# Attention maxima paced two groups ahead with the mask added on VectorE, and retention's dependent steps one projection part later

## The chip, the cores and the metric

The kernel runs on one core of a Trainium2 chip. The metric is device time in microseconds (us) of one launch, the median of three runs; one further run was profiled, and every row below is from it. The engines are named as the profile names them: PE (TensorE matmul; PEld is its weight load), DVE (VectorE), ACT (ScalarE), POOL (GpSimd) and SP, which issues all DMAs.

## What is computed

One decoder layer on 2048 tokens of width 1024, in float32: RMSNorm and one input projection; 8 heads of chunkwise retention beside 8 heads of causal softmax attention with low-rank q and k/v; one output projection with residual; RMSNorm, up-projection, causal depthwise convolution, SiLU gate, down-projection with residual; a last RMSNorm. The two parts that the change touches are, cut short:

```python
# retention, per head and chunk
scores = einsum('bnihd,bnjhd->bnhij', q, k) * decay_mask
o = einsum('bnhij,bnjhe->bnihe', scores, v) + einsum('bnihd,bnhde,hi->bnihe', q, r_prev, xi)
# then group norm over each head and the gate silu(g) * o

# attention, per block of queries
s = (q_nope . k_nope + q_pe . k_pe) * scale
s = where(key_pos <= q_pos, s, finfo(float32).min)
p = softmax(s)                       # needs the maximum of every row of s
o = einsum('bhqk,bkhd->bqhd', p, v)
```

## The kernel before, in words

Every float32 operand is split into a rounded high part and a low part, and a product is three matmuls (`mm3`: high by high, high by low, low by high, lines L72 to L74). Splits are made by ACT (high part, L64) and by POOL or DVE (low part, L68).

The program has four stretches. First norm, latents and the q, k, v rows of attention, which go to HBM. Then retention and attention side by side: this is the stretch that the change touches. Then the output projection, and last the convolution MLP. The scheduler of the language reorders the instructions of each engine by readiness and by the order in which the code emits them; the order that it leaves is fixed in the program.

**Retention** (`ret_stream`, `ret_chunk`) works on 4 head pairs times 8 chunks of 256 tokens, two pairs interleaved. A chunk has 8 projection parts of 6 matmuls (L72 to L74, tile `pm`, one PSUM bank), four for each 128 tokens, and after each four parts DVE rotates q and k out of the bank (L597, L598, L600). Then come 8 dependent steps: the split of q and k (tile `S`, ACT and POOL) with 16 half-size transposes on PE (L619, tile `x`); two score steps (L635, L636, mask L637, split `SC`); two output steps (L661, reduced by L662 into `o`); the state (L671 to L678); the statistics of the norm with the gate (L684, L686 `o<-o,sg`, the small operations L104 to L114, L687); and the two transposes of `o` with the store (L691). The dependent steps of a chunk are emitted between the projection parts of the next chunk, one after each part, the first step after the first part.

**Attention** (`att_stream`, `att_max`, `att_group`) has 32 groups: 8 heads times 4 groups g of 512 queries. `att_max` finds the maxima of a group's rows: 4(g+1) units, each a matmul q by k into the single bank `sm` (L727) and a DVE reduction of that bank (L731). Where the unit holds the diagonal, a second matmul of `unit` and a mask adds the mask in PSUM first (L730). Then the maxima are negated (L734), split (L66, L68), transposed into `sm` (L740) and copied by ACT into rows 96 and 97 of the group's `q` tile (L741), so that the score matmul subtracts them. `att_group` then walks over 4g+4 blocks of 128 keys: scores into `s` (two banks, L759 to L764), two exponentials on ACT (L766, L767), the low part on DVE (L768), the running denominator on POOL (`den`, L773, L777), and two value matmuls (L782, L783). At a group's end POOL adds the output halves (L815, tile `ot`) and splits `den`, and two small matmuls sum it (L788, also in `sm`). A chunk of k and v is loaded and split (ACT and POOL, tiles `k`, `v`) when the first maximum unit needs it.

While group n runs, the maxima of group n+1 are emitted between its steps at the rate units/steps:

```python
            steps, units = 4 * g + 5, 4 * groups[n + 1][1] + 6 if n + 1 < len(groups) else 0
            owed, qn = 0.0, None
            for c in self.att_group(h, g, q):
                owed += units / steps
```

that is 2.0 a step in the group g=0, 1.56 in g=1, 1.38 in g=2 and 0.35 in g=3, whose successor is the small first group of the next head. `side_by_side` interleaves the two streams by their estimated costs; four retention chunks go with one head of attention.

Of the kernel before, what the change touches and what calls it, by code (L numbers as in the profile page):

```python
# [20 lines left out]
P = 128  # L21
D = 1024
# [22 lines left out]


AHEAD = 2
RET_SHARE = .91
ATT_SHARE = .6
LEAD = 9  # L50
# [3 lines left out]
class Block:  # L54
# [387 lines left out]

    def att_pools(self, ctx):
        nc, a, tc = self.nc, self.a, self.tc
        self.kp = ctx.enter_context(tc.tile_pool(name="ak", bufs=5, side="right"))
        self.b1 = b1 = ctx.enter_context(tc.tile_pool(name="a1", bufs=1, side="right"))
        self.b2 = ctx.enter_context(tc.tile_pool(name="a2", bufs=2, side="right"))
        self.b3 = ctx.enter_context(tc.tile_pool(name="a3", bufs=3, side="right"))
        self.pa_m = ctx.enter_context(tc.tile_pool(name="pa_m", bufs=1, space=PSUM, side="right"))
        self.pa_s = ctx.enter_context(tc.tile_pool(name="pa_s", bufs=2, space=PSUM, side="right"))  # L450
        self.pa_o = ctx.enter_context(tc.tile_pool(name="pa_o", bufs=1, space=PSUM, side="right"))
        self.unit = b1.tile([P, P], F32R, name="unit")
        nc.scalar.activation(self.unit, self.ident, AF.Copy)
        m = b1.tile([P, 640], F32R, name="mqk")
        r = self.raw.tile([P, D], F32, name="raw")[:, :640]
        nc.sync.dma_start(r, a["mask_att"])
        nc.scalar.activation(m, r, AF.Copy)
        self.mkq, self.mqk = m[:, 0:384], m[:, 256:640]
        self.ones = b1.tile([P, 2], F32R, name="ones")
        nc.vector.memset(f32(self.ones), 1.0)  # L460

        self.vts = [b1.tile([P, 4, 160], F32R, name=f"v{i}") for i in range(5)]
# [53 lines left out]

    def ret_stream(self):
        nc, a = self.nc, self.a
        hs, pend = {}, None

        def load(ch):
            if ch < 8 and ch not in hs:
                t = hs[ch] = []
                for tt in range(2):
                    h = self.hp.tile([P, 2, KC, P], F32R, name="h")
                    nc.sync.dma_start(f32(h), f32(self.hT_s[2 * ch + tt]))
                    t.append(h)

        for p in (0, 2):
            load(0)  # L530
            for ch in range(8):
                load(ch)
                for j in range(2):
                    if p + j not in self.Wr:
                        for k in range(4):
                            self.ret_weights(p + j, k)
                    it = self.ret_chunk(p + j, ch, self.Wr[p + j], hs[ch])
                    for _ in range(8):
                        yield next(it)
                        if pend is not None:  # L540
                            yield next(pend, 0)
                    if ch == 7:
                        self.next_weights(p + j)
                    if pend is not None:
                        for c in pend:
                            yield c
                    pend = it
                hs.pop(ch)
        for c in pend:
            yield c  # L550

    def att_stream(self):
        groups = [(h, g) for h in range(H) for g in range(4)]
        q = None
        for c, q in self.att_max(*groups[0]):
            yield c
        for n, (h, g) in enumerate(groups):
            nxt = self.att_max(*groups[n + 1]) if n + 1 < len(groups) else iter(())
            steps, units = 4 * g + 5, 4 * groups[n + 1][1] + 6 if n + 1 < len(groups) else 0
            owed, qn = 0.0, None  # L560
            for c in self.att_group(h, g, q):
                owed += units / steps
                while owed >= 1:
                    owed -= 1
                    m = next(nxt, None)
                    if m:
                        c += m[0]
                        qn = m[1]
                yield c
            for m in nxt:  # L570
                qn = m[1]
                yield m[0]
            q = qn
        self.finish()
        yield 450

    def ret_chunk(self, p, ch, W, hs):
        nc, c1, c2, px = self.nc, self.r1, self.r2, self.pr_x
        mm = nc.tensor.matmul
        qk = c2.tile([P, 2, 4, 64], F32, name="qk")  # L580
        vg = c2.tile([P, 2, 256], F32, name="vg")
        V = c2.tile([P, 2, 2, 2, 64], F32R, name="V")
        sg = c2.tile([P, 2, P], F32, name="sg")
        for tt in range(2):
            tok = 2 * ch + tt
            ps = self.pr_m.tile([P, 512], F32, name="pm")
# [18 lines left out]
        th = c1.tile([P, 2, P], F32, name="th")  # L605
# [35 lines left out]
        if ch:  # L641
# [6 lines left out]
        o = c2.tile([P, 4, 64], F32, name="o")  # L648
        for ib in range(2):

            ps = px.tile([P, 512], F32, name="x")
            for x in range(2):
# [12 lines left out]
                axis=AX, op=ALU.add)  # L665
# [12 lines left out]
            nc.vector.tensor_tensor(R, pv[:, :, 64:128], R, op=ALU.add)  # L678
        yield 440

        sq = c1.tile([P, 4, 64], F32, name="gsq")
# [31 lines left out]
    def att_max(self, h, g):  # L713

        nc, b2 = self.nc, self.b2
        q = b2.tile([98, 2, 512], F32R, name="q")
# [3 lines left out]
        mx = b2.tile([P, 4, 4], F32, name="mx")  # L720
# [12 lines left out]
        nm = b2.tile([P, 4], F32, name="nm")  # L733
        nc.vector.tensor_reduce(nm, mx[:, :, :g + 1], axis=AX, op=ALU.max, negate=True)  # L734
# [663 lines left out]
```

## Time and profile before

| | us |
|---|---|
| median of 3 runs | 2969.17 (2965.57 to 2970.82) |
| the profiled run's own time | 2968.21 |
| its span in the trace | 2966.4 |
| PE busy | 2768.4 (93%) |
| DVE busy | 1953.1 (66%) |
| POOL busy | 1957.8 (66%) |
| ACT busy | 1348.3 (45%) |
| PE share of the chain that ended last | 56%, DVE 15%, ACT 7%, POOL 6% |

The span begins with the first instruction and ends with the last; the run's own time has 1.8 us around it. A matmul is pipelined, so its duration is longer than the distance to the next one, and the distance is what it costs. "PEclk" is the share of the full TensorE clock of 2.4 GHz that was granted in a stretch; the lower level is 1.2 GHz.

### The profile page before, as it was taken

What the parts mean: (1) busy time and instruction counts of PE and PEld (TensorE: products, weight loads), DVE (VectorE), ACT (ScalarE), POOL (GpSimd) and SP (SyncE); (2) the same over time, 40 slices, a digit from 0 to 9 for tenths busy, and PEclk for the clock granted to TensorE, in tenths of its full rate; (3) what the DMA queues carried; (4) which work ended last, traced back from release to release, by engine and by line L of the source; (5) the groups of instructions that cost most, each with busy time, mean ns of one, the idle gap of its engine ahead of it and who ended that gap; (6) DMA issues with size and microseconds to landing.
All of it is one profiled execution on the core that took longest, in us unless ns stands there. A gap on an engine that the chain in (4) does not pass through costs nothing.

```text
span 2966.4 us, 37611 instructions
## 1 busy us (share of the span) xinstructions
PE 2768.4 (93%) x12800; PEld 2237.1 (75%) x12800; DVE 1953.1 (66%) x3265; ACT 1348.3 (45%) x2544; POOL 1957.8 (66%) x1478
## 2 busy tenths in 40 slices
PE   7998999988999999989899999989995999999998
PEld 6976777777777777767787777778874888887887
DVE  8765676667666666754458888844266888887243
ACT  5435656555655555551333333333334433333343
POOL 2035656566655556663599999765558999995564
PEclk9999999999999999999899999989997999999999
DMA  7663112223211121326622222264552222224453
GB/s 259 219 209 95 53 55 65 59 70 97 63 54 55 54 65 45 97 88 196 241 94 77 73 85 81 79 228 153 187 192 96 71 79 86 79 74 163 149 193 109
DMA packets 153360, 332.91 MB, mean 112 GB/s; under 512 B 35016, under 2 KB 68296, under 8 KB 147024
## 3 DMA queue, kind: packets, MB, share of 16 engines
q1 hardware_dynamic: 153168, 330.51, 34.1%
q8 instruction: 101, 1.65, 0.2%
q14 instruction: 91, 0.75, 0.1%
HBM read 237.71 MB, written 92.75 MB: 111 GB/s over the span
## 4 chain that ended last, share of the span: by engine, by line
PE 56%; DVE 15%; ACT 7%; issue 6%; POOL 6%; DMA 3%; SPq 0%; POOLq 0%; ACTq 0%; DVEq 0%
PE b L74 10%; PE b L73 10%; PE b L72 10%; PE pm L74 3%; PE pm L72 3%; PE pm L73 3%; DVE w L1137 2%; DVE u L1131 2%; DVE w L1138 2%; PE sm L727 2%; ACT w L1136 2%; PE s L759 2%; PE x L661 2%; DVE w L1163 2%; PE s L764 1%
## 5 line engine op out<-in xcount | busy, mean ns | idle before, releaser
L68 POOL TENSOR_TENSOR w<-raw,w 128x512 fp32r<-128x512 f32 (+2 forms) x315 | 523.2, 1676 | 256.2 <-ACT w L64 243.8
L74 PE MATMUL b<-F,w 128*128 128x512 f32 x1232 | 492.5, 400 | 0.0
L72 PE MATMUL b<-F,w 128*128 128x512 f32 x1232 | 487.7, 396 | 3.8 <-DVE u L1131 3.8
L73 PE MATMUL b<-F,w 128*128 128x512 f32 x1232 | 487.5, 396 | 3.1 <-POOL F L68 3.1
L777 POOL TENSOR_TENSOR den<-den,pc 128x512 f32<-128x512 f32 (+2 forms) x256 | 294.1, 1149 | 207.8 <-ACT pc L766 189.8
L64 ACT ACTIVATE w<-raw 128x512 fp32r<-128x512 f32 (+2 forms) x328 | 214.4, 658 | 348.1 <-PE b L74 179.0
L72 PE MATMUL b<-w 128*128 128x512 f32 x832 | 330.2, 397 | 21.0 <-DVE u L1131 13.0
L74 PE MATMUL b<-w 128*128 128x512 f32 x832 | 328.1, 394 | 1.6 <-POOL w L68 1.5
L73 PE MATMUL b<-w 128*128 128x512 f32 x832 | 328.0, 394 | 0.0
L731 DVE TENSOR_REDUCE mx<-sm 128x1 f32<-128x512 f32 (+2 forms) x320 | 194.1, 607 | 173.8 <-PE sm L727 126.9
L68 DVE TENSOR_TENSOR w<-xr,w 128x512 fp32r<-128x512 f32 x88 | 110.4, 1255 | 284.9 <-ACT w L64 284.9
L72 PEld LDWEIGHTS b<-F,w 128*128 128x128 f32 x1232 | 232.6, 189 | 65.7 <-DVE u L1131 11.0
L73 PEld LDWEIGHTS b<-F,w 128*128 128x128 f32 x1232 | 232.5, 189 | 62.4 <-POOL F L68 3.5
L74 PEld LDWEIGHTS b<-F,w 128*128 128x128 f32 x1232 | 232.4, 189 | 54.5
L768 DVE TENSOR_TENSOR pc<-s,pc 128x512 fp32r<-128x512 f32 (+1 forms) x320 | 197.6, 619 | 99.6 <-ACT s L767 74.6
L1136 ACT ACTIVATE w<-u,cw 128x1024 f32<-128x1024 f32 x88 | 109.5, 1244 | 333.1 <-DVE u L1131 198.5
L1137 DVE SCALAR_TENSOR_TENSOR w<-u,cw,w 128x1024 f32<-128x1024 f32 x88 | 165.7, 1883 | 128.7 <-ACT w L1136 128.7
L766 ACT ACTIVATE pc<-s 128x512 fp32r<-128x512 f32 (+1 forms) x320 | 172.6, 539 | 148.5 <-PE s L764 142.1
L72 PE MATMUL pm<-w,h 128*128 128x512 f32 x512 | 211.1, 412 | 6.3 <-DVE t L598 4.8
L68 POOL TENSOR_TENSOR w<-xr,w 128x512 fp32r<-128x512 f32 x110 | 204.6, 1872 | 9.4 <-ACT w L64 9.4
L74 PE MATMUL pm<-w,h 128*128 128x512 f32 x512 | 206.5, 403 | 0.0
L73 PE MATMUL pm<-w,h 128*128 128x512 f32 x512 | 205.7, 402 | 0.0
(263 smaller groups left out, 6618.6 us busy)
## 6 DMA issues: line engine op xcount, KB each, us to landing
raw<-in_w_down SPq DMA_DIRECT2D x88, 512.0 KB
h<-hT_s SPq DMA_DIRECT2D x32, 1024.0 KB
xr<-in_w_up SPq DMA_DIRECT2D x44, 512.0 KB
raw<-in_w_up SPq DMA_DIRECT2D x44, 512.0 KB
g_s<-w SPq DMA_DIRECT2D x44, 512.0 KB
xr<-g_s SPq DMA_DIRECT2D x88, 256.0 KB
hT_s<-hT SPq DMA_DIRECT2D x16, 1024.0 KB
raw<-in_w_ret SPq DMA_DIRECT2D x16, 512.0 KB
```

Of the source, the lines that this page charges most:

```text
L64: nc.scalar.activation(hi, src, AF.Copy)
L68: eng.tensor_tensor(lo, src, f32(hi), op=ALU.subtract)
L72: mm(out, lhsT=lh, rhs=rh, start=start, stop=False)
L73: mm(out, lhsT=lh, rhs=rl, start=False, stop=False)
L74: mm(out, lhsT=ll, rhs=rh, start=False, stop=stop)
L661: mm(ps[:, x * P:x * P + 256], lhsT=l, rhs=r, start=n == 0, stop=n == len(ops) - 1)
L731: nc.vector.tensor_reduce(mx[:, i, c:c + 1], ps[:, :w], axis=AX, op=ALU.max)
L766: nc.scalar.activation(pc[:, 0, r0:], ps[:, r0:], AF.Exp, scale=ATT_SCALE)
L768: nc.vector.tensor_tensor(pc[:, 1, r0:], ps[:, r0:], f32(pc[:, 0, r0:]), op=ALU.subtract)
L777: nc.gpsimd.tensor_tensor(den[:, r0:], den[:, r0:], hi[:, r0:], op=ALU.add)
L1136: nc.scalar.activation(acc, x[:, 2:1026], AF.Identity, scale=w2, bias=b)
L1137: nc.vector.scalar_tensor_tensor(acc, x[:, 1:1025], w1, acc, op0=ALU.mult, op1=ALU.add)
```

## The change

Four edits. (1) `att_max`: the mask matmul goes; on diagonal units DVE adds the mask and takes the maximum in one `tensor_tensor_reduce`, which writes the sum back to the bank. The mask for it is a float32 tile, filled by a POOL memset and a DMA. (2) `att_stream`: the maxima become one stream over all groups, taken at 1.1 units a step, up to two groups ahead; what a group still lacks at its start is emitted there. `q` and `mx` get three buffers, `k` and `v` six. (3) `ret_stream`: nothing of the chunk before is emitted after the first part, its steps follow after parts 2 to 8, and its last step after part 3 of the chunk after. (4) `ret_chunk`: `qk`, `vg`, `V`, `sg` and `o` go from two buffers to one, and the squares share a tile with `th`.

```diff
+MAX_PACE = 1.1
...
-        self.kp = ctx.enter_context(tc.tile_pool(name="ak", bufs=5, side="right"))
+        self.kp = ctx.enter_context(tc.tile_pool(name="ak", bufs=6, side="right"))
...
+        self.mqk = b1.tile([P, 512], F32, name="mqk")
+        nc.gpsimd.memset(self.mqk, 0.0)
+        nc.sync.dma_start(self.mqk[:, 384:512], a["mask_att"][:, 384:512])
...
-                    for _ in range(8):
+                    for n in range(8):
                         yield next(it)
-                        if pend is not None:
+                        if n and pend is not None:
                             yield next(pend, 0)
+                        if n == 2 and old is not None:
+                            yield next(old, 0)
                     if ch == 7:
                         self.next_weights(p + j)
-                    if pend is not None:
-                        for c in pend:
-                            yield c
-                    pend = it
+                    old, pend = pend, it
...
     def att_stream(self):
         groups = [(h, g) for h in range(H) for g in range(4)]
-        q = None
-        for c, q in self.att_max(*groups[0]):
-            yield c
+        qs, done = {}, set()
+        def maxima():
+            for n, hg in enumerate(groups):
+                while n > self.at + 2:
+                    yield 0
+                for c, qs[n] in self.att_max(*hg):
+                    yield c
+                done.add(n)
+        self.at, mx, owed = 0, maxima(), 0.0
         for n, (h, g) in enumerate(groups):
-            nxt = self.att_max(*groups[n + 1]) if n + 1 < len(groups) else iter(())
-            steps, units = 4 * g + 5, 4 * groups[n + 1][1] + 6 if n + 1 < len(groups) else 0
-            owed, qn = 0.0, None
-            for c in self.att_group(h, g, q):
-                owed += units / steps
+            self.at = n
+            while n not in done:
+                yield next(mx)
+            for c in self.att_group(h, g, qs.pop(n)):
+                owed = min(owed + MAX_PACE, 2.0)
                 while owed >= 1:
                     owed -= 1
...
-        qk = c2.tile([P, 2, 4, 64], F32, name="qk")
+        qk = c1.tile([P, 2, 4, 64], F32, name="qk")
...
-                nc.tensor.matmul(ps[:, :N], lhsT=q[0:96, 0, i * P:(i + 1) * P], rhs=k[0:96, 0, :N], start=True, stop=c < g)
+                nc.tensor.matmul(ps[:, :N], lhsT=q[0:96, 0, i * P:(i + 1) * P], rhs=k[0:96, 0, :N], start=True, stop=True)
                 if c == g:
-                    m = self.mqk[:, 0:256] if w > P else self.mqk[:, P:384]
-                    nc.tensor.matmul(ps[:, N - 256:N], lhsT=self.unit, rhs=m, start=False, stop=True)
-                nc.vector.tensor_reduce(mx[:, i, c:c + 1], ps[:, :w], axis=AX, op=ALU.max)
+                    nc.vector.tensor_tensor_reduce(ps[:, :w], ps[:, :w], self.mqk[:, 512 - w:], scale=1.0, scalar=-3.0e38, op0=ALU.add, op1=ALU.max, accum_out=mx[:, i, c:c + 1])
+                else:
+                    nc.vector.tensor_reduce(mx[:, i, c:c + 1], ps[:, :w], axis=AX, op=ALU.max)
```

The line numbers of the changed kernel are 5 higher in these functions (L619 is L624 there, L686 is L691, L731 is L736). Three places of the order show what moves.

**PE, ahead of a chunk's transposes.** The rows that end at the first transpose of the same retention chunk; tile `w_2159` holds the weights of the next chunk's first projection part, `w_2193` those of its second. Before:

```order
L72 MATMUL pm_4675<-w_2159,h_4291 128x512
L73 MATMUL pm_4675<-w_2159,h_4291 128x512
L727 MATMUL sm_4661<-k_4561,q_4496 128x256
L730 MATMUL sm_4661<-mqk_2435,unit_2433 128x256
L74 MATMUL pm_4675<-w_2159,h_4291 128x512
L759 MATMUL s_4682<-q_4165,k_3979 128x512
L760 MATMUL s_4682<-q_4165,k_3979 128x512
L764 MATMUL s_4682<-q_4165,k_3979 128x512
L782 MATMUL o2_4485<-pc_4607,v0_2441 128x512
L783 MATMUL o3_4486<-pc_4607,v0_2441 96x512
L727 MATMUL sm_4693<-k_3510,q_4496 128x512
L619 MATMUL x_4707<-ident_73,S_4696 128x128
```

In the changed kernel:

```order
L75 MATMUL pm_4636<-w_2193,h_4265 128x512
L73 MATMUL pm_4636<-w_2193,h_4265 128x512
L732 MATMUL sm_4657<-k_4067,q_4377 128x512
L74 MATMUL pm_4636<-w_2193,h_4265 128x512
L75 MATMUL pm_4636<-w_2193,h_4265 128x512
L764 MATMUL s_4666<-q_4023,k_3678 128x512
L765 MATMUL s_4666<-q_4023,k_3678 128x512
L769 MATMUL s_4666<-q_4023,k_3678 128x512
L787 MATMUL o2_4496<-pc_4604,v5_2449 128x512
L788 MATMUL o3_4497<-pc_4604,v5_2449 96x512
L732 MATMUL sm_4677<-k_4461,q_4377 128x384
L624 MATMUL x_4691<-ident_73,S_4680 128x128
```

The transposes now stand behind the second part instead of the first: 31 matmuls lie between the last projection matmul of their own chunk and them, where 22 did.

**DVE, where the first group of the second head begins.** The rows that end at the gate's product of the same retention chunk. Before:

```order
L768 TENSOR_TENSOR pc<-s,pc 128x256
L731 TENSOR_REDUCE mx<-sm 128x1
L662 TENSOR_REDUCE o<-x 128x128
L731 TENSOR_REDUCE mx<-sm 128x1
L734 TENSOR_REDUCE nm<-mx 128x4
L66 CAST n_4118<-nm 128x4
L68 TENSOR_TENSOR n_4118<-nm,n_4118 128x4
L662 TENSOR_REDUCE o<-x 128x128
L731 TENSOR_REDUCE mx<-sm 128x1
L768 TENSOR_TENSOR pc<-s,pc 128x512
L684 TENSOR_REDUCE gs_4239<-gsq 128x4
L686 TENSOR_TENSOR o<-o,sg 128x256
```

In the changed kernel:

```order
L734 ISA sm,mx<-sm,mqk 128x128
L734 ISA mx 128x1
L736 TENSOR_REDUCE mx<-sm 128x1
L667 TENSOR_REDUCE o<-x 128x128
L773 TENSOR_TENSOR pc<-s,pc 128x256
L736 TENSOR_REDUCE mx<-sm 128x1
L734 ISA sm,mx<-sm,mqk 128x256
L734 ISA mx 128x1
L667 TENSOR_REDUCE o<-x 128x128
L736 TENSOR_REDUCE mx<-sm 128x1
L689 TENSOR_REDUCE gs_4249<-th 128x4
L691 TENSOR_TENSOR o<-o,sg 128x256
```

Each masked maximum is two instructions now (`ISA`), the second of which writes the 128x1 result, and the negation and split of the maxima no longer stand here; the gate's product is still emitted as the first group of a head begins.

**POOL, at the same place.** Before:

```order
L777 TENSOR_TENSOR den<-den,pc 128x256
L68 TENSOR_TENSOR q<-raw,q 96x512
L68 TENSOR_TENSOR pc<-den,pc 128x512
L815 TENSOR_TENSOR ot<-ot,otl 64x512
L68 TENSOR_TENSOR k<-raw,k 98x512
L68 TENSOR_TENSOR v_2443<-raw,v_2443 128x4x64
L773 TENSOR_TENSOR den<-pc 128x512
L645 TENSOR_TENSOR G<-R_94,gst 128x128
```

In the changed kernel:

```order
L69 TENSOR_TENSOR q<-raw,q 96x512
L69 TENSOR_TENSOR pc<-den,pc 128x512
L69 TENSOR_TENSOR k<-raw,k 98x512
L69 TENSOR_TENSOR v_2445<-raw,v_2445 128x4x64
L820 TENSOR_TENSOR ot<-ot,otl 64x512
L778 TENSOR_TENSOR den<-pc 128x512
L650 TENSOR_TENSOR G<-R_94,gst 128x128
```

The same operations follow one another, with the splits of `k` and `v` ahead of the addition into `ot` instead of behind it.

## Rows read from the trace of the kernel before

**Rows 1.** Windows: length, busy time (instructions) of PE, PEld, DVE, ACT, POOL, then PEclk

```profile
240.00:1314.00 1074.00, 990.90 (x5022) 790.88 (x5021) 725.59 (x1580) 632.88 (x1319) 642.86 (x638) 0.97 0.22 65
1314.00:2966.00 1652.00, 1569.67 (x6735) 1266.92 (x6734) 1061.02 (x1177) 607.19 (x977) 1259.42 (x786) 0.97 0.38 126
```

**Rows 2.** PE's waits from 240 to 1315: waiter, releaser, total us, times, longest

```profile
PE sm L727 <- DVE mx L731: 21.9, 19, 2.4
PE x L619 <- POOL S L68: 15.9, 17, 1.6
PE s L759 <- DVE pc L768: 9.7, 9, 3.5
PE sm L788 <- DVE mx L731: 9.2, 3, 3.4
PE s L759 <- ACT q L741: 8.4, 7, 1.9
```

**Rows 3.** PEld's waits there: the same edges seen at the weight load

```profile
PEld x L619 <- POOL S L68: 23.6, 18, 2.0
...
PEld s L759 <- ACT q L741: 15.0, 22, 2.1
```

**Rows 4.** PE timeline, back to back: start, duration; at PEclk 1.0, then after 384

```profile
708.48 0.28 PE L635 MATMUL x<-Q,K 128*128 128x256 f32 x1
708.59 0.28 PE L636 MATMUL x<-Qs,K 128*128 128x256 f32 x1
...
708.95 0.40 PE L72 MATMUL pm<-w,h 128*128 128x512 f32 x1
709.18 0.40 PE L73 MATMUL pm<-w,h 128*128 128x512 f32 x1
...
385.36 0.63 PE L74 MATMUL pm<-w,h 128*128 128x512 f32 x1
385.79 0.63 PE L72 MATMUL pm<-w,h 128*128 128x512 f32 x1
```

**Rows 5.** Timeline of POOL, DVE and PE at the start of the second head

```profile
376.64 1.29 POOL L68 TENSOR_TENSOR k<-raw,k 98x512 fp32r<-98x512 f32 x1 [0.65 <-ACT k L64]
376.75 3.38 DVE L686 TENSOR_TENSOR o<-o,sg 128x256 f32<-128x256 f32 x1
377.88 0.73 POOL L68 TENSOR_TENSOR v<-raw,v 128x256 fp32r<-128x256 f32 x1
378.57 1.28 POOL L773 TENSOR_TENSOR den<-pc 128x512 f32<-128x512 f32 x1
...
381.72 0.68 DVE L731 TENSOR_REDUCE mx<-sm 128x1 f32<-128x512 f32 x1
...
382.45 0.39 PE L727 MATMUL sm<-k,q 96*128 96x256 f32 x1 [2.41 <-DVE mx L731]
```

**Rows 6.** Windows around that place and seven like it, two shown, and their sum

```profile
376.70:390.00 13.30, 10.22 (x40) 7.41 (x38) 11.36 (x24) 5.52 (x14) 7.00 (x9) 0.87 0.24 58
512.50:526.00 13.50, 11.09 (x39) 8.11 (x38) 11.55 (x24) 5.73 (x14) 7.20 (x9) 0.75 0.23 63
...
sum 108.10, PE 84.40 PEld 61.36 DVE 90.38 ACT 50.23 POOL 60.97; mean PE 10.55 PEld 7.67 DVE 11.30 ACT 6.28 POOL 7.62
```

**Rows 7.** DVE lines: durations in ns, minimum, median, maximum

```profile
L686 DVE TENSOR_TENSOR o<-o,sg x32: 412/416/4106, 225.8 to 1307.7; 128x256 f32<-128x256 f32 x32
L637 DVE TENSOR_TENSOR x<-x,mask x64: 421/423/433, 219.4 to 1301.9; 128x256 f32<-128x256 f32 x64
L734 DVE TENSOR_REDUCE nm<-mx x32: 147/155/170, 245.0 to 1280.0; 128x4 f32<-128x4 f32 x8, 128x4 f32<-128x8 f32 x8, 128x4 f32<-128x12 f32 x8, 128x4 f32<-128x16 f32 x8
```

**Rows 8.** DVE groups by shape, 240 to 1314: busy us, mean ns of one, idle before

```profile
L731 DVE TENSOR_REDUCE mx<-sm 128x1 f32<-128x512 f32 x224 | 153.7, 686 | 132.1 <-PE sm L727 126.9 <-PE sm L730 4.1
L768 DVE TENSOR_TENSOR pc<-s,pc 128x512 fp32r<-128x512 f32 x222 | 152.0, 685 | 61.9 <-ACT s L767 59.7 <-POOL S L68 1.6
```

**Rows 9.** POOL group: busy us, mean ns of one, idle before

```profile
L815 POOL TENSOR_TENSOR ot<-ot,otl 64x512 f32<-64x512 f32 x31 | 39.8, 1285 | 56.0 <-ACT otl L814 56.0
```

More of the change, by code (lines that the diff above doesn't have):

```diff
@@ L453, in att_pools @@
         nc.scalar.activation(self.unit, self.ident, AF.Copy)
-        m = b1.tile([P, 640], F32R, name="mqk")
-        r = self.raw.tile([P, D], F32, name="raw")[:, :640]
-        nc.sync.dma_start(r, a["mask_att"])
+        m = b1.tile([P, 384], F32R, name="mkq")
+        r = self.raw.tile([P, D], F32, name="raw")[:, :384]
+        nc.sync.dma_start(r, a["mask_att"][:, 0:384])
         nc.scalar.activation(m, r, AF.Copy)
-        self.mkq, self.mqk = m[:, 0:384], m[:, 256:640]
+        self.mkq = m[:, 0:384]
+        self.mqk = b1.tile([P, 512], F32, name="mqk")
+        nc.gpsimd.memset(self.mqk, 0.0)
+        nc.sync.dma_start(self.mqk[:, 384:512], a["mask_att"][:, 384:512])
         self.ones = b1.tile([P, 2], F32R, name="ones")
         nc.vector.memset(f32(self.ones), 1.0)
-        self.vts = [b1.tile([P, 4, 160], F32R, name=f"v{i}") for i in range(5)]
+        self.vts = [b1.tile([P, 4, 160], F32R, name=f"v{i}") for i in range(6)]
         for v in self.vts:
@@ L518, in ret_stream @@
         nc, a = self.nc, self.a
-        hs, pend = {}, None
+        hs, pend, old = {}, None, None
         def load(ch):
@@ L537, in ret_stream @@
                     it = self.ret_chunk(p + j, ch, self.Wr[p + j], hs[ch])
-                    for _ in range(8):
+                    for n in range(8):
                         yield next(it)
-                        if pend is not None:
+                        if n and pend is not None:
                             yield next(pend, 0)
+                        if n == 2 and old is not None:
+                            yield next(old, 0)
                     if ch == 7:
                         self.next_weights(p + j)
-                    if pend is not None:
-                        for c in pend:
-                            yield c
-                    pend = it
+                    old, pend = pend, it
                 hs.pop(ch)
-        for c in pend:
+        for c in (*old, *pend):
             yield c
@@ L553, in att_stream @@
         groups = [(h, g) for h in range(H) for g in range(4)]
-        q = None
-        for c, q in self.att_max(*groups[0]):
-            yield c
-        for n, (h, g) in enumerate(groups):
-            nxt = self.att_max(*groups[n + 1]) if n + 1 < len(groups) else iter(())
-            steps, units = 4 * g + 5, 4 * groups[n + 1][1] + 6 if n + 1 < len(groups) else 0
-            owed, qn = 0.0, None
-            for c in self.att_group(h, g, q):
-                owed += units / steps
+        qs, done = {}, set()
[7 more added lines that the diff above has]
+        self.at, mx, owed = 0, maxima(), 0.0
+        for n, (h, g) in enumerate(groups):
+            self.at = n
[3 more added lines that the diff above has]
+                owed = min(owed + MAX_PACE, 2.0)
                 while owed >= 1:
                     owed -= 1
[L565 to L568, printed above, removed]
+                    c += next(mx, 0)
                 yield c
[L570 to L573, printed above, removed]
         self.finish()
@@ L579, in ret_chunk @@
         mm = nc.tensor.matmul
-        qk = c2.tile([P, 2, 4, 64], F32, name="qk")
-        vg = c2.tile([P, 2, 256], F32, name="vg")
-        V = c2.tile([P, 2, 2, 2, 64], F32R, name="V")
-        sg = c2.tile([P, 2, P], F32, name="sg")
+        qk = c1.tile([P, 2, 4, 64], F32, name="qk")
+        vg = c1.tile([P, 2, 256], F32, name="vg")
+        V = c1.tile([P, 2, 2, 2, 64], F32R, name="V")
+        sg = c1.tile([P, 2, P], F32, name="sg")
         for tt in range(2):
@@ L647, in ret_chunk @@
             rst = Rst.rearrange("p h a d -> p (h a d)")
-        o = c2.tile([P, 4, 64], F32, name="o")
+        o = c1.tile([P, 4, 64], F32, name="o")
         for ib in range(2):
@@ L679, in ret_chunk @@
         yield 440
-        sq = c1.tile([P, 4, 64], F32, name="gsq")
+        sq = c1.tile([P, 2, P], F32, name="th").rearrange("p a (b d) -> p (a b) d", d=64)
         nc.scalar.activation(sq, o, AF.Square, scale=0.125)
@@ L715, in att_max @@
         nc, b2 = self.nc, self.b2
-        q = b2.tile([98, 2, 512], F32R, name="q")
+        q = self.b3.tile([98, 2, 512], F32R, name="q")
         r = self.raw.tile([P, D], F32, name="raw")
@@ L719, in att_max @@
         self.split(q[0:96, 0], q[0:96, 1], r[0:96, 0:512])
-        mx = b2.tile([P, 4, 4], F32, name="mx")
+        mx = self.b3.tile([P, 4, 4], F32, name="mx")
         for i in range(4):
```

## The prediction

> **What bounds the kernel now.** I read the windows first, for the stretch in which retention and attention run together: 1074 us, PE busy for 990.9 of them, so PE idles for 83.1 us, and the granted clock is 0.97 [rows 1]. The other engines have room (DVE 726, POOL 643, ACT 633 us), so PE's own work and its waits set this stretch. The 240 us ahead of it and the 1652 us behind run code that the change does not touch, and I leave them as they are.
>
> Then the list of PE's waits in that stretch, to see what is late. Three edges lead: a maximum matmul waits for DVE to free the one `sm` bank (21.9 us, and 9.2 us where the denominator's matmul wants the same bank), the transposes of retention wait for POOL's low part of `S` (15.9 us, 17 times, so about 0.9 us each), and a score matmul waits for `q`'s last rows from ACT (8.4 us) or for a score bank (9.7 us) [rows 2]. Seen at the weight load, before the matmuls still in flight are counted as busy, the transposes' wait is 23.6 us and `q`'s 15.0 [rows 3].
>
> Last the timeline around the longest waits. At 376.75 DVE's gate product takes 3.38 us, while POOL runs the splits of `k` and `v` and a `den` addition without a gap (376.64 to 379.85); the maximum behind it on DVE is done only at 382.4, and the next `sm` matmul has waited 2.41 us [rows 5]. The same product takes 0.416 us at the median and 4.1 at the longest [rows 7]. Such a place stands once in every head, because four retention chunks go with one head: eight windows around them hold 108.1 us with 84.4 us of PE, so 23.7 us of the 83.1 idle [rows 6]. The clock falls there too: five of the eight windows are granted 0.87 to 0.89 and three 0.74 to 0.76, as the two shown. That is 5 x 13.5 x 0.125 + 3 x 13.6 x 0.25, about 18.7 us of full clock lost, of 1074 x 0.03 = 32 us in the stretch [rows 1, 6]. At the lower level a 512-column matmul costs 0.43 us instead of 0.23 [rows 4].
>
> **The change, part by part.**
>
> *The mask matmuls go.* There are 4 in each of 32 groups, 128 of 256 columns. Four such matmuls back to back took 708.48 to 708.95, so 0.117 us each [rows 4]: 15 us of PE work, on the engine that bounds. **-15** (0 would need PE to wait anyway at each; with a half of them behind waits, -8).
>
> *The transposes come one part later.* Behind them now lie six more projection matmuls at 0.23 us and the attention matmuls between, nine more matmuls in the order shown, at least 1.4 us. The waits average 0.9 us and the longest is 1.6 on PE and 2.0 at the weight load [rows 2, 3]. All but one or two should go. What is late next in that chain, the score steps, keeps its distance of one part. I take **-17**, between 15.9 and 23.6 less a remainder; bounds -12 and -22. The single buffers cost nothing that I see: `qk`, `vg`, `V` and `sg` are read by steps after part 2 and written again after part 4, and `o` is transposed after part 3 and written again after part 5. Cover gone, each of 32 chunks would wait a DVE or ACT operation of about 0.4 us, 13 us in all.
>
> *The maxima come ahead.* A group's `q` rows are then copied at least some steps before its first score, except in the first head, where 1.1 units a step do not keep up with a larger group behind and 3 or 4 units are emitted on their own. The 8.4 us (15.0 at the weight load) go: **-10**, bounds -5 and -14.
>
> *The even pace.* The 23.7 us of the eight windows are waits for `sm`, but for one of 3.5 us for a score bank [rows 2, 6]; so 20 of the 31.1 us that `sm` waits on DVE lie there and 11 outside. Before, a group g=0 takes two units a step and g=1 1.56; now it is 1.1. In the order, maxima that stand fewer than 6 matmuls behind the one before are 74 of 384 users of the bank, where they were 90: the scheduler had spread them already. **-7**, bounds 0 and -10.
>
> *The clock outside the eight windows.* 13 us are lost there [rows 1, 6] beside 59 us of idle; the items above take away about 34 of these, and I give the clock the same share: **-8**, bounds 0 and -12.
>
> *The eight places.* The gate product still stands where a head's first group begins, and POOL still runs `pc`, `k`, `v`, `ot` and `den` there, now in a closer row. I see no reason for it to be held less: **0**. If it misses POOL's row, 23.7 + 18.7 = 42 us go; if `k`, `v`, `ot` and `den` hold it for 1.29 + 0.73 + 1.29 + 1.28 = 4.6 us instead of 3.4 [rows 5, 9], each place costs 1.2 us more, 10 us, with the clock up to 18.
>
> *The masked maximum.* DVE's nearest rows: a product of a PSUM and an SBUF operand into PSUM takes 0.426 us for 256 columns, and a difference of a PSUM and an SBUF operand 0.685 for 512, where the plain maximum takes 0.686 [rows 7, 8]. So the main instruction should cost what the reduction does. The second one, 128x1, is at most like the small reduction of 0.155 us [rows 7]: 128 x 0.155 = 20 us of DVE, of which 348 us are idle. It delays PE only where `sm` is waited for, and then frees the bank later; a quarter of 128 gives 5. **+5**, bounds 0 and +20. Were the new instruction to take two cycles for each column, 128 x 0.33 us = 43 us of DVE, about half in front of a waiting `sm`, +21.
>
> The trace shows that these PSUM operations are not held by POOL: the product with the mask spreads from 421 to 433 ns, the gate product with two SBUF operands from 412 to 4106 [rows 7]. The Trainium skill, SBUF — State Buffer, "Who interferes with whom", says why: a VectorE instruction with two SBUF inputs shares a read interface with GpSimd and is blocked for whole instructions, one with at most one SBUF input is not. By that rule the masked maximum is safe and the gate product is not, as the trace agrees.
>
> One rule speaks against the change. VectorE: DVE Perf Modes, "Rules for kernel authors", in the Trainium skill, asks to minimise the count of operations, and its section on two Vector instructions with no wait says that an accumulator output makes a second instruction; by the page's (N+151)/0.96 ns the 128 read-outs would be an estimated 20 us of DVE. Were all of it in front of PE, the sum would be 15 us worse.
>
> *Start.* The mask tile now needs a POOL memset and a DMA before the first maximum, and the first head's extra units stand bare: **+4**, bounds 0 and +8.
>
> Sum: -15 - 17 - 10 - 7 - 8 + 0 + 5 + 4 = -48. The profiled run took 2968.2 us, 1.0 below the median; from the median that is **2921 us**.
>
> **The rivals.**
>
> *The eight places dissolve* (0.20). The product is emitted one part later, and the row on POOL has another order; a shift of 3 us is enough to miss it. For it: the median product is not held at all [rows 7]. Against: the order shows both still at the head's start. 2921 - 42 = 2879 us.
>
> *DVE eats half of it* (0.20). The masked maximum is slower than its neighbours' rows say (+16 over the sum) or PE's waits move from POOL and ACT to the `sm` bank (half of the 34 us of waits come back, +17). Then 2937 to 2954, say 2945 us. For it: DVE was 68% busy in the stretch and has 128 instructions more in less time. This is also where the rule on the count of operations leads.
>
> *The change does not pace* (0.05). The order's counts (74 of 90) say that the scheduler decides the spacing; then the pace and its clock give nothing, and only masks, transposes and `q` stay: -38, near 2932 us.
>
> *POOL's row holds DVE at more places* (0.08): slower. Each place now costs (23.7 + 18.7) / 8 = 5.3 us. The gate product comes with each of 32 chunks; if it also met a closed row on POOL at other group ends, 10 more places would eat the 48 us, and 16 more (three in each head) give +85, 3006 us. Against: only the end of a head's last group brings `pc`, `k`, `v`, `ot` and `den` together.
>
> **How the numbers follow.** The forecast itself has 0.47, with its own range 2900 to 2940. From 2876, where the places dissolve, to 2954, the end of DVE's case, leaves out the slower rival and some of the tails. A measurement of this kernel tells a change of 0.2%, 6 us, from none. Faster by more: all cases but the last and a tail of DVE's case, 0.88; within: 0.04; slower: 0.08.
>
> **What would show it.** In the changed profile: no line with `sm<-mqk,unit`; the wait of the `x` transposes on `S` under 3 us; the wait of `s` on `q` under 2; two DVE lines for the masked maximum, of about 0.43 us at 256 columns and under 0.2; the gate product with about eight durations over 2.5 us, and a granted clock of 0.97 to 0.98 in a stretch that is some 48 us shorter; the stretch behind it within 5 us of 1652. The prediction is wrong if the gate product is held at other places than one a head, if the masked maximum takes over 0.6 us at 256 columns, or if waits for `sm` grow past 31 us.

## The result and the profile after

The changed kernel takes 2931.85 us (median of 4 runs, 2930.57 to 2933.8) where the kernel before took 2969.99 beside it: ratio 0.9877, 95% interval [0.9865, 0.989]. That is 37 us faster; 48 were forecast.

The windows of the changed kernel, for the stretches that answer to [rows 1] (columns as there):

```profile
240.00:1278.00 1038.00, 958.62 (x4894) 773.85 (x4893) 744.36 (x1708) 632.28 (x1321) 647.83 (x639) 0.98 0.22 66
1278.00:2930.00 1652.00, 1568.30 (x6738) 1265.50 (x6737) 1059.99 (x1178) 608.23 (x979) 1261.09 (x787) 0.97 0.38 127
```

All of the gain lies in the stretch of retention and attention, 1074 to 1038 us; behind it nothing moved. PE's busy time fell there by 32 us, but its idle time only from 83.1 to 79.4 us. So waits that went were replaced by others. PE's waits in that stretch, which answer to [rows 2], with two more rows of the kernel before, for the transposes of the maxima, ahead of them:

```profile
PE sm L740 <- DVE n L68: 3.2, 7, 0.7
...
PE sm L740 <- DVE r_g L109: 1.4, 1, 1.4
```

```profile
PE sm L732 <- DVE mx L736: 18.2, 17, 5.2
PE sm L745 <- DVE n L69: 18.2, 11, 2.7
PE sm L732 <- ACT otl L795: 6.7, 10, 1.0
PE s L764 <- DVE pc L773: 4.7, 5, 2.4
PE sm L732 <- DVE mx L734: 4.2, 6, 1.0
PE pm L73 <- DVE r_g L115: 3.8, 1, 3.8
PE sm L793 <- DVE z_g L108: 3.8, 1, 3.8
...
PE sm L793 <- ACT s L772: 2.2, 2, 1.1
...
PE x L624 <- POOL S L69: 1.9, 1, 1.9
...
PE sm L793 <- DVE r_g L110: 1.7, 2, 0.8
PE s L764 <- ACT q L746: 1.2, 1, 1.2
```

Two waits went as forecast: the transposes on `S` (15.9 to 1.9 us) and the scores on `q` (8.4 to 1.2). The maxima wait for the bank as long as before (18.2 and 4.2, where it was 21.9). New are 15 us in which the transposes of the negated maxima wait for the two instructions that split them (`n`, L67 and L69), 6.7 us in which the bank is still read by ACT for a denominator (`otl`), and three single waits of 3.8, 3.8 and 5.2 us (the last is part of the 18.2). The 9.2 us in which a denominator's matmul waited for the maxima [rows 2] are gone. Added up over all its users, the matmuls that write the bank `sm` waited 35.7 us before and wait 55.0 now.

The changed kernel's VectorE rows, by shape, and then two lines' instructions with the least, median and longest ns:

```profile
L736 DVE TENSOR_REDUCE mx<-sm 128x1 f32<-128x512 f32 x192 | 131.7, 686 | 64.7 <-PE sm L732 63.4
L734 DVE CUSTOM_DVE_ANT_0 sm<-sm,mqk 128x512 f32<-128x512 f32 x32 | 22.2, 695 | 9.5 <-PE sm L732 9.3
L734 DVE DVE_READ_ACCUMULATOR2_ANT mx<- 128x1 f32 x128 | 18.0, 141 | 0.0
...
L734 DVE CUSTOM_DVE_ANT_0 sm<-sm,mqk 128x256 f32<-128x256 f32 x32 | 13.7, 428 | 3.8 <-PE sm L732 3.2
```

```profile
L691 DVE TENSOR_TENSOR o<-o,sg x32: 410/416/1254, 227.4 to 1271.3; 128x256 f32<-128x256 f32 x32
```

```profile
L67 DVE CAST n<-nm x32: 157/214/2171, 245.0 to 1239.1; 128x4 fp32r<-128x4 f32 x32
L69 DVE TENSOR_TENSOR n<-nm,n x32: 146/165/2414, 245.2 to 1239.3; 128x4 fp32r<-128x4 f32 x32
```

The masked maximum costs what its neighbours' rows said: 428 ns at 256 columns, 695 at 512 beside 686 for the plain one, and 141 ns for the read-out. The gate product, up to 4106 ns before [rows 7], is no longer held over 1254, where eight took over 2.5 us before: the eight places are gone in that form. The small split is held in their stead, up to 2171 and 2414 ns for work of 157 and 146; 11 of its 32 copies take over 1 us, where 6 did before. The timeline of one such place, VectorE and then GpSimd (start, us, instruction):

```profile
456.36 0.15 DVE L739 TENSOR_REDUCE nm<-mx 128x4 f32<-128x4 f32 x1
456.43 0.41 DVE L612 SCALAR_TENSOR_TENSOR sg<-th,vg 128x256 f32<-128x256 f32 x1
456.76 1.25 DVE L67 CAST n<-nm 128x4 fp32r<-128x4 f32 x1
458.04 1.18 DVE L69 TENSOR_TENSOR n<-nm,n 128x4 fp32r<-128x4 f32 x1
```

```profile
456.59 1.39 POOL L69 TENSOR_TENSOR S<-qk,S 128x512 fp32r<-128x512 f32 x1 [1.08 <-ACT S L65]
457.94 1.26 POOL L782 TENSOR_TENSOR den<-den,pc 128x512 f32<-128x512 f32 x1
```

Each of the two ends just when a GpSimd instruction ends (457.98, 459.20): 0.3 us of work takes 2.4, and PE waits at 459.28. The 5.2 us wait is the same thing with a longer row on GpSimd, six operations without a gap (`k`, `den`, `S`, `V`, `v`, `den`, 919.33 to 925.85). VectorE in that time:

```profile
920.94 2.17 DVE L114 SCALAR_TENSOR_TENSOR z_g<-z_g 128x4 f32<-128x4 f32 x1
923.03 1.02 DVE L612 SCALAR_TENSOR_TENSOR sg<-th,vg 128x256 f32<-128x256 f32 x1
923.97 1.90 DVE L115 SCALAR_TENSOR_TENSOR r_g<-z_g,r_g 128x4 f32<-128x4 f32 x1
925.90 0.43 DVE L692 TENSOR_TENSOR o<-o,r_g 128x256 f32<-128x256 f32 x1
926.25 0.68 DVE L736 TENSOR_REDUCE mx<-sm 128x1 f32<-128x512 f32 x1
```

The maximum that PE waits for stands behind three held instructions of the norm; it was not held itself.

### The profile page after: what moved, and what is told of

It reads as the page before. It is cut to its first block, busy times and chain, and to the rows that moved or that the text cites. A ratio compares the mean times of both kernels' runs of the same rounds, so it can differ in the third digit from the quotient of the medians.

```text
span 2930.5 us, 37500 instructions
## 1 busy us (share of the span) xinstructions
PE 2732.9 (93%) x12672; PEld 2217.2 (76%) x12672; DVE 1972.3 (67%) x3393; ACT 1347.0 (46%) x2544; POOL 1962.2 (67%) x1480
## 4 chain that ended last, share of the span: by engine, by line
PE 42%; DVE 10%; issue 5%; ACT 3%; POOL 2%; DMA 2%; SPq 0%; ACTq 0%; DVEq 0%; POOLq 0%
PE b L75 12%; PE b L74 12%; PE b L73 12%; DVE w L1142 2%; ACT w L1141 2%; DVE u L1136 2%; DVE w L1143 1%; DVE w L1168 1%; DMA raw<-mixa_s 1%; DVE w L1167 1%; PE x L666 1%; ACT u L1166 1%; POOL w L69 1%; PE pm L75 1%; PE pm L74 1%
## 5 line engine op out<-in xcount | busy, mean ns | idle before, releaser
L69 POOL TENSOR_TENSOR w<-raw,w 128x512 fp32r<-128x512 f32 (+2 forms) x315 | 523.5, 1677 | 251.1 <-ACT w L65 239.3
L69 DVE TENSOR_TENSOR w<-xr,w 128x512 fp32r<-128x512 f32 x88 | 108.6, 1234 | 286.3 <-ACT w L65 286.3
L73 PE MATMUL pm<-w,h 128*128 128x512 f32 x512 | 209.1, 408 | 12.2 <-DVE r_g L115 3.8
L69 POOL TENSOR_TENSOR w<-xr,w 128x512 fp32r<-128x512 f32 x110 | 205.5, 1881 | 9.4 <-ACT w L65 9.4
L74 PE MATMUL pm<-w,h 128*128 128x512 f32 x512 | 203.9, 398 | 0.0
L73 PEld LDWEIGHTS b<-w 128*128 128x128 f32 x832 | 158.6, 191 | 59.4 <-DVE u L1136 16.8
L75 PE MATMUL pm<-w,h 128*128 128x512 f32 x512 | 203.1, 397 | 0.0
```

What stands on the lines that cost most here:

```text
L69: eng.tensor_tensor(lo, src, f32(hi), op=ALU.subtract)
L73: mm(out, lhsT=lh, rhs=rh, start=start, stop=False)
L74: mm(out, lhsT=lh, rhs=rl, start=False, stop=False)
L75: mm(out, lhsT=ll, rhs=rh, start=False, stop=stop)
```

## The experiments

The theory after this reading: the mask and the shift pay as forecast; the paced stream gives back most of what it gains, because the short split between a group's last maximum and its transposes is held by GpSimd. The rivals: the shift (or the stream) alone is worth the eight places, 42 us; the masked maximum is what eats the gain; the pace itself is wrong.

Three kernels do one edit alone, three leave one out. Differences below are ratio minus 1, times 2969 us; an interval is 3 to 6 us to either side. The single buffers go with the shift and with the stream, and no kernel has them alone.

**Mask alone.** The kernel before, with only

```diff
-                    nc.tensor.matmul(ps[:, N - 256:N], lhsT=self.unit, rhs=m, start=False, stop=True)
+                    nc.vector.tensor_tensor_reduce(ps[:, :w], ps[:, :w], self.mqk[:, 512 - w:], ...)
```

> The kernel before with the mask edit alone: no mask matmul, the masked maximum on VectorE. By the terms of the prediction -15 for 128 matmuls and +5 for the second instruction, so about -10 (2960 us); the gate product is still held over 2.5 us at about eight places, since nothing around it has moved. Rival: VectorE gives the gain back on the sm bank (0.49 us + 0.14 us for a masked maximum of 256 columns in the changed kernel's trace against 0.686 us for the plain one of 512): within 3 us of before, with PE's wait of sm on mx longer than the 21.9 us of before.

Measured: 2959.25 us, ratio 0.9965 [0.9952, 0.9978], -10 us. The product is still held (longest 2925 ns), though four times over 2.5 us and not about eight, and the wait of `sm` on the plain maximum is 20.6 us. In the stretch PE's busy time falls by 13 us and its idle time grows by 4, so the mask's two terms, -15 and +5, hold; the rival that the masked maximum gives all back falls. (The 0.49 us in the expectation is the median over all four widths; 256 columns take 428 ns.)

**Shift alone.** The kernel before, with the single buffers and

```diff
-                        if pend is not None:
+                        if n and pend is not None:
                             yield next(pend, 0)
+                        if n == 2 and old is not None:
+                            yield next(old, 0)
```

> The kernel before with retention's dependent steps one part later and the single buffers, maxima and mask as before. If the eight held gate products are a matter of where retention's steps fall against GpSimd's row, they go here: -17 for the transposes and about -42 for the eight places, near -59 (2910 us), with the longest gate product under 1.5 us. If it is the paced maxima that dissolve them, this kernel keeps seven or more gate products over 2.5 us and gains -17 to -25 (2944 to 2952 us). In both cases the wait of the x transposes on S falls from 15.9 us to under 3.

Measured: 2950.46 us, 0.9935 [0.992, 0.9951], -19 us. The product is free, as one theory wanted, and the gain is the other's:

```profile
L686 DVE TENSOR_TENSOR o<-o,sg x32: 414/416/1249, 227.7 to 1287.7; 128x256 f32<-128x256 f32 x32
```

```profile
PE sm L727 <- DVE mx L731: 19.3, 17, 2.7
...
PE x L619 <- POOL S L68: 2.5, 2, 1.5
```

So it is the shift that takes the product out of GpSimd's row. The 9.2 us of the denominators go with it, but the maxima's own wait hardly falls (21.9 to 19.3), their transposes wait 7.3 us for the split instead of 3.2, and the projection matmuls, which write the bank `pm`, wait 14.4 us where they waited 4.5. The timeline of a head's start in this kernel shows why, VectorE and then GpSimd:

```profile
391.17 1.21 DVE L114 SCALAR_TENSOR_TENSOR r_g<-z_g,r_g 128x4 f32<-128x4 f32 x1
392.41 1.45 DVE L687 TENSOR_TENSOR o<-o,r_g 128x256 f32<-128x256 f32 x1
393.78 0.41 DVE L731 TENSOR_REDUCE mx<-sm 128x1 f32<-128x256 f32 x1
```

```profile
391.08 1.28 POOL L68 TENSOR_TENSOR S<-qk,S 128x512 fp32r<-128x512 f32 x1
392.32 1.25 POOL L777 TENSOR_TENSOR den<-den,pc 128x512 f32<-128x512 f32 x1
```

This place is still there; other instructions of the same norm now stand in it, and the maximum is late behind them.

**Stream alone.** The kernel before, with the new `att_stream`, its buffers, and the single buffers that make room for them.

```diff
-                owed += units / steps
+                owed = min(owed + MAX_PACE, 2.0)
```

> The kernel before with the paced stream two groups ahead (and the single buffers that make room for it), mask matmuls and retention's place as before. If the stream dissolves the eight places: no gate product over 2.5 us and -35 to -55 (2915 to 2935 us). If the shift does: the eight stay, the waits of s on q go (-10), and the new waits of the row transposes on the split of the negated maxima (about 20 us at the changed kernel's places, three of before) eat that: between -5 and +10 (2964 to 2979 us).

Measured: 2962.53 us, 0.998 [0.997, 0.9991], -6 us, just below the -5 to +10 that the second theory gave. The product stays held (longest 2603 ns, three times over 2.5 us and 13 times over 1), and the waits show the trade:

```profile
PE sm L729 <- DVE mx L733: 26.6, 22, 2.7
...
PE sm L729 <- ACT otl L792: 11.9, 12, 1.4
PE sm L742 <- DVE n L69: 9.2, 6, 2.7
```

The scores' waits, on `q` and on a free bank, go from 18.1 to 5.6 us, and the waits of all matmuls that write `sm` from 35.7 to 54.2. PE's idle time grows by 5 us in all. What the kernel gains goes with the clock, granted 0.98 instead of 0.97 in the stretch: PE is busy for 977 us with the same matmuls, 991 before.

**Without the stream** (mask and shift). The changed kernel, with the old `att_stream` and its buffers:

```diff
-                owed = min(owed + MAX_PACE, 2.0)
+                owed += units / steps
```

> The changed kernel with the maxima emitted as before (one group ahead, at the rate units/steps), mask and shift kept. If the shift dissolves the eight places and the new waits for sm come from the stream, this is faster than the changed kernel by some 10 us (2915 to 2925 us), with PE's waits of the row transposes back under 4 us. If the stream dissolves the eight places, it is slower than the changed kernel: -10 and -20, near 2940 us, with the held gate products back.

Measured: 2916.18 us, 0.982 [0.9806, 0.9833], -53 us. It beats the changed kernel by 17 us by the ratios, and its waits in the stretch are

```profile
PE sm L743 <- DVE n L68: 10.5, 15, 1.6
PE sm L730 <- DVE mx L734: 10.3, 15, 2.0
...
PE sm L730 <- ACT otl L793: 1.8, 4, 0.8
```

with no wait longer than 2.4 us. The split's wait did not go back under 4 us, so it is not the stream's own.

**Without the shift** (mask and stream), and **without the mask** (shift and stream):

```diff
-                        if n and pend is not None:
+                        if pend is not None:
```

> The changed kernel with retention's steps back in their old place (mask and stream kept). The shift alone gave -19, and -43 on top of the mask alone. If the shift is worth what the transposes waited, this is 17 to 20 us slower than the changed kernel (2949 to 2952), with the x transposes waiting over 14 us for S. If with the stream the shift dissolves nothing more than that and the stream costs 15 by itself, the same; if shift and mask act on the eight places together whatever the maxima do, it is near 2959 + 8, 2965 us.

```diff
+                    nc.tensor.matmul(ps[:, N - 256:N], lhsT=self.unit, rhs=m, start=False, stop=True)
-                    nc.vector.tensor_tensor_reduce(...)
```

> The changed kernel with the mask matmuls back and the plain maximum (shift and stream kept). If the mask edit is worth what it is alone (-10), this is near 2942 us. If it is the mask together with the shift that frees the head starts, also under the stream, it is some 20 to 30 us slower than the changed kernel, 2952 to 2962 us.

Measured: 2958.21 us, 0.9956 [0.9943, 0.9968], for the first; 2938.91 us, 0.9908 [0.9888, 0.9928], for the second. Without the shift the kernel is 23 us slower than the changed one, between the two sums that were expected, and the transposes wait 20.7 us for `S`; without the mask it is 9 us slower, about what the mask is worth alone, with intervals that just overlap. All combinations, with three columns from the traces for the stretch of retention and attention (240 us to the last transpose of retention): PE's idle time, and the waits of all matmuls that write `sm` and of all that write the score banks `s`, added up from the wait rows, in us:

| edits | us less than before | sum of the single edits | PE idle | waits, `sm` | waits, `s` |
|---|---|---|---|---|---|
| none (before) | | | 83 | 35.7 | 18.1 |
| mask | 10 | | 87 | 37.5 | 18.7 |
| shift | 19 | | 68 | 29.1 | 16.7 |
| stream | 6 | | 88 | 54.2 | 5.6 |
| mask, stream | 13 | 16 | 92 | 59.6 | 5.4 |
| shift, stream | 27 | 25 | 70 | 46.1 | 3.1 |
| mask, shift, stream (the change) | 37 | 36 | 79 | 55.0 | 5.9 |
| mask, shift | 53 | 30 | 50 | 23.7 | 7.5 |

The change comes out at the sum of its three edits, but not because they leave each other alone. Mask with shift is 24 us better than their sum, and the stream on top of it loses 17. The two columns at the right say by what: in each of the four pairs the stream adds 17 to 31 us of waits at `sm`, and it takes away 12 to 14 us of waits at `s` in three of them; where mask and shift are in already, only 7.5 us are left there, and it takes away 1.6.

**The split one unit earlier**, and **the split from the bank**. The changed kernel; the second line is the second kernel's, in place of a tile in SBUF:

```diff
+                if i == 3 and c == g:
+                    nm = ps[:, 0:4]
+                    nc.vector.tensor_reduce(nm, mx[:, :, :g + 1], axis=AX, op=ALU.max, negate=True)
...
                 yield 213, q
```

> The changed kernel with the negated maxima and their split emitted one unit earlier, still from SBUF. If the 18.2 us that the row transposes wait for the split come from emission distance, they fall under 6 us and the kernel gains about 10 us (2922). If the split is held by GpSimd's rows wherever it stands (0.16 us at its least, up to 2.2 us in the changed kernel), several of its 32 copies still last over 1 us and the time stays within 5 us of 2931.9.

> As the run that emits the split one unit earlier, but the negated maxima lie in four columns of the sm bank just read, so that each of the split's two instructions has an operand in PSUM. If GpSimd's rows are what holds the split, none of the 64 instructions lasts over 0.5 us, the wait of the row transposes falls under 5 us, and the kernel gains 8 to 14 us (2918 to 2924). Rival: the bank is now kept some 0.5 us longer, 32 times, and the waits of the next sm matmul grow by what is gained: within 4 us of 2931.9.

Measured: 2929.12 us, 0.9861 [0.9848, 0.9875], not told from the changed kernel; the copy's longest is still 2.17 us and 9 of the 32 still take over 1 us, though the wait fell to 12.2. From the bank: 2921.88 us, 0.9833 [0.9819, 0.9846], 10 us (by the ratios 13) less than the changed kernel, with

```profile
L67 DVE CAST n<-sm x32: 144/161/165, 245.8 to 1226.6; 128x4 fp32r<-128x4 f32 x32
L69 DVE TENSOR_TENSOR n<-sm,n x32: 149/161/164, 246.0 to 1226.8; 128x4 fp32r<-128x4 f32 x32
```

and 0.9 us of waits for it. None of the 64 instructions is held, and the longer use of the bank hardly shows (its wait on the plain maximum is 17.5 us); PE's idle time falls by 13 us, less than the 17 of that wait, since small waits grew elsewhere (on `S` from 1.9 to 4.4). The two kernels differ only in where the split's source lies, so it is the source in SBUF, and not distance, that lets the split be held. That GpSimd's work there is what holds it is read from timelines like the one above, where the held instruction ends as one of GpSimd's does.

**The same without the stream.** Mask and shift with the split from the bank.

> Mask and shift without the stream (2916.2 us), with the split from the sm bank. Its row transposes wait 10.5 us for the split, 15 times. By the theory of holds -6 to -10 (2906 to 2910); by the rival (bank kept longer) no change, 2912 to 2920.

Measured: 2909.37 us, 0.9797 [0.9783, 0.981], -60 us, about 7 us under the same without this edit, whose interval just overlaps.

**A higher pace.** The changed kernel, with

```diff
-MAX_PACE = 1.1
+MAX_PACE = 2.0
```

> The changed kernel with up to 2.0 units a step in place of 1.1, still two groups ahead at most. If the low even pace costs (the row transposes of a group come late, and the denominator's and the maxima's users of the sm bank meet), this gains some 8 to 16 us, toward the kernel without the stream (2916). If what costs is being two groups ahead (the k and v splits of a head away from its start), it stays within 4 us of 2931.9; if bursts cost, as the change supposes, it is slower, by 7 or more.

Measured: 2989.06 us, 1.0079 [1.0062, 1.0097], 60 us slower than the changed kernel by the ratios. The row transposes' wait is 25.6 us, the two of the maxima are 21.2 and 13.6, and all matmuls that write `sm` wait 74.4 together. Counted on PE in the traces, which may lack a few records, some 320 of 384 uses of the bank now stand fewer than ten matmuls behind the one before, where the changed kernel has some 150. So a higher pace in the stream costs, far more than expected, and a low pace is not what the stream loses by. How closely the uses follow is not the whole of it: the kernel before and the one with mask and shift have some 190 such uses and wait less for the bank than the changed kernel.

**Halves on GpSimd.** The changed kernel, and the one just above without the stream, with GpSimd's 512-column operations cut in two, as in

```diff
-        eng.tensor_tensor(lo, src, f32(hi), op=ALU.subtract)
+        for c in (slice(0, n), slice(n, None)):
+            self.nc.gpsimd.tensor_tensor(lo[:, c], src[:, c], f32(hi[:, c]), op=ALU.subtract)
```

> The changed kernel with GpSimd's 512-column operations of the stretch (den, the low parts of S, k, q and of the denominator, ot) as two instructions of half the size. In the changed kernel a held VectorE instruction mostly lasts until one GpSimd instruction ends (1.2 us). If that is how it is held, the holds become 0.6 us, the waits of sm on DVE (40.6 us in the three leading rows) lose a third, and the kernel gains 8 to 15 us (2917 to 2924). Rival: VectorE does not get in at the added ends (the gate product of before was held through three GpSimd instructions), and GpSimd only gets longer: 0 to +10 us.

> Mask and shift without the stream, split from the sm bank (2909.4 us), with the halves as well. If holds last for one GpSimd instruction, -4 to -10 (2899 to 2905); by the rival 0 to +10 (2909 to 2919).

Measured: 2923.03 us, 0.9852 [0.9835, 0.987], some 7 us under the changed kernel by the ratios, whose intervals just overlap; and 2907.35 us, 0.9803 [0.9788, 0.9817], not told from the kernel without the halves. The wait of the row transposes fell from 18.2 to 10.3 us, and one copy of 32 takes over 1 us where 11 did. But single holds got longer: the copy's 2922 ns (282.83 to 285.75) end with the last of five GpSimd instructions in a row (`q`, `pc` twice, `ot` twice, to 285.72), and a `z_g` takes 4.6 us. VectorE gets in at many of the added ends and misses others. Inconclusive as an improvement.

## Why the prediction was right, and where a term was off

**The sum: -48 forecast, -37 measured, and in part by luck.** The number is near because two errors cancel. Mask and shift together, with the start, were put at -15 - 17 + 5 + 4 = -23 and their share of the clock; they measured -53. The stream was put at -10 - 7 and its share; in the change it costs 17.

**Mask: -15 and +5, measured -10.** Right, with the instruction times too: the 128 read-outs took 18.0 us of DVE, of which 20 were expected. The +4 for the start was not needed: the first `sm` matmul starts at 240.21 us, 239.95 before.

**Shift: -17, measured -19** with its share of the clock. Right, and in the main for the reason given: the transposes' wait went from 15.9 to 2.5 us. The denominators' 9.2 us that went too were not in the term, nor were the waits of the projection matmuls, 4.5 to 14.4 us. "The single buffers cost nothing that I see" is open: the stream alone has them too and shows no wait at `pm`, so they do not bring it by themselves, but no run has the shift without them.

**Maxima ahead -10, even pace -7: measured -6 for both alone.** This is the term that was mis-sized. The `q` waits fell by 7.2 us as said, but they fell from 7.3 to 1.5 with mask and shift as well, without the stream. The step that failed is "20 of the 31.1 us that `sm` waits on DVE lie there and 11 outside ... -7": it counted the bank's old waits, and not that the same bank has other users, the row transposes, which wait 15 us more for their split, and ACT's read of a denominator, for which the maxima wait 6.7. The runs show the waits at this bank rise with the stream, by 17 to 31 us in the four pairs of the table, where a fall was forecast. The sign "if waits for `sm` grow past 31 us" came true by all users (35.7 to 55.0), not by the two that it was taken from: the maxima's and the denominators' waits on DVE went from 31.1 to 27.9.

**Clock -8:** the granted clock went from 0.97 of 1074 us to 0.98 of 1038, so from about 32 us lost to 21, -11. About as forecast, though not told apart by place.

**The eight places, 0.** Near in sum by luck, and wrong as told. "About eight durations over 2.5 us" was expected of the gate product and none is over 1254 ns; the rival that they dissolve came true for the product, but its 42 us did not follow in the change, where the norm's other instructions and the split are held. The price belonged to GpSimd's row and whatever PE needs behind it on VectorE, not to that product. The mechanism of the slower rival, holds at more places, was at work as well, at a smaller size: 18.2 us for the split and 12.8 in the three single waits.

**The rule on the two engines.** The prediction took from the Trainium skill, SBUF — State Buffer, "Who interferes with whom", that a VectorE instruction with at most one SBUF input is not blocked. Here the copy `n<-nm`, with one input, took up to 2171 ns, and 165 at most when that input lay in PSUM. The section excepts instructions in the modes that use both ports, and names copies and casts among those that can enter them; with that half of the rule, which the prediction left out, the trace agrees. No row tells in which mode the copy ran. The section also says that whoever issues first has the shared ports for the whole instruction and the other is blocked; the rows show a block that outlasts one instruction: 2.17 us for `z_g` through the end of one addition and a whole `S`.

**What stays open.** Why mask and shift together gain 24 us more than apart. Where they do is in the rows: against the shift alone, PE idles 18 us less, mostly in the waits at `s` (16.7 to 7.5) and at `sm` (29.1 to 23.7). One place of it can be followed. At the same head's start the maximum ends as late behind its matmul in both kernels, 2.9 us (391.27 to 394.19) with the shift alone and 3.1 (383.84 to 386.93) with both; but the trace has 4 matmuls of other work on PE between it and the bank's next user in the first, and 12 in the second, so PE waits 2.05 us there and 0.67 here. Waits of over 1.2 us for the maxima stand at six heads' starts in the first kernel and at one in the second. So the order that the scheduler leaves seems to decide; that is argued, since no run moved it alone, and the scores' waits were not followed. Also, with the split out of SBUF in both, the stream still loses 11 us. The three single waits of 3.8 to 5.2 us, which the kernel without the stream does not have, are about that much, but no run took them away alone.

## What to carry to other kernels

Price a change of order edit by edit, but list the waits by resource and not by instruction: here all users of one PSUM bank, and all that stands behind one held instruction. A small VectorE operation between two steps of the critical engine is worth keeping out of SBUF when GpSimd is busy there: four columns of a PSUM bank already at hand were worth some 7 to 13 us. A single change that measures well, and near its forecast, may still hold an edit that costs; leaving out each in turn found 17 us here.

## What the runs showed of the hardware

A one-input copy of 4 columns lasts 157 ns at its least and up to 2171 beside GpSimd's work in SBUF (the changed kernel), and never over 165 with its input in PSUM (the split from the bank); where GpSimd has six operations in a row, three VectorE instructions in it took 5.1 us for some 0.7 of work. The masked maximum with its read-out cost 428 and 141 ns at 256 columns, and neither was ever held: the longest at 256 columns is 433 ns, and the longest of 128 read-outs 144.
